# Gate and up of three feed-forwards as seven block products, token-major, in a two-layer hybrid decoder trunk

## The chip, the cores and the metric

One core of a Trainium2 chip runs the whole program as one launch. The metric is the device time of one execution in microseconds (us); the comparisons use medians of runs. The engines are TensorE (PE, matmuls; PEld is its weight load), VectorE (DVE), ScalarE (ACT), GpSimd (POOL) and SyncE (SP), which here only issues DMAs. Each works through its own queue in order and waits for the others by semaphores.

## The reference

Two layers over 512 tokens of width 1024, all in float32. The change concerns `swiglu_ffn`, which runs twice per layer:

```python
for l in range(DEPTH):                                   # DEPTH = 2
    h = rmsnorm(x, ffn1_norm[l])
    x = x + 0.5 * swiglu_ffn(h, ffn1_w_gate[l], ffn1_w_up[l], ffn1_w_down[l])
    h = rmsnorm(x, mix_norm[l])                          # S5 scan, pooling, convolution
    ...
    x = x + y @ w_out[l]
    h = rmsnorm(x, xattn_norm[l])
    x = x + cross_attention(h, rmsnorm(mem, mem_norm[l]), ...)
    h = rmsnorm(x, ffn2_norm[l])
    x = x + 0.5 * swiglu_ffn(h, ffn2_w_gate[l], ffn2_w_up[l], ffn2_w_down[l])
return rmsnorm(x, final_norm)

def swiglu_ffn(h, w_gate, w_up, w_down):                 # 1024 -> 2816 -> 1024
    return (jax.nn.silu(h @ w_gate) * (h @ w_up)) @ w_down
```

## The kernel before

Every float32 product is made of three matmuls on rounded parts (`mm3`, L249 to L252): high x high, high x low and low x high. The high part of a tile is a copy on ACT, the low part a subtraction on DVE. `wload` (L237) does that for weights: a DMA on SP's queue into `raw` (three buffers), a copy to `wh` (L241) and a subtraction to `wl` (L243) on DVE, or on POOL where `eng` says so.

`Norm` (L165) makes the input of each stage. `half` (L183) is called when half a token tile of x is final: a square with a sum on ACT, the mean on DVE (L190), the power -1/2 on POOL (L191, one column), then `emit` (L195): the gain product on DVE (L197), four 128x128 transposes on PE (L200) into a bank of the pool `ax` (two banks), and the high and low parts (L201 on ACT, L202 on DVE). `prep` loads the gain. The result is x transposed: 128 rows of the width by 512 tokens, eight of them.

`ffn` (L320) goes over the 22 column tiles of 128 of the inner width. `gate_up` (L326) keeps a 128x128 block of weights still and moves 512 tokens: 8 blocks of the width x 3 passes for the gate (`pgffn`) and the same for up (`puffn`). The first tile does it by halves of the tokens (`proj_halves`, 256 columns), so that it can begin when two token tiles are normed. Sigmoid, two multiplications (L336 to L338) and a split (L257, L259) give h, with the inner width on the partitions, as `down` (L341) needs it: in three passes of 6 tiles, token tiles of h stay still and 512 columns of the down weights move (`pdffn`), and the sum is added to x on DVE (L317). The last 4 tiles go in `finish` (L353, `plffn`), token tile by token tile, so that the next norm starts on tile 0 while PE is on tile 1.

The stages run in the order ffn1, mix, att, ffn2 for each layer. The S5 matrices of a layer are built in the background of its own ffn1 (`s5_build`, L377), for the most part on POOL, into twelve tiles of the pool C, which the mixer reads. PSUM has 8 banks: 5 in the pool `mm`, 2 in `ax`, 1 named `cacc`. Order within each engine's queue is set when the program is built: a planner takes the instructions that its own model of time holds ready, those that come earlier in the program first, and gives them buffers from the pools.

Of the kernel before, what the change touches and what calls it, by code (L numbers as in the profile page):

```python
# [9 lines left out]
F32 = mybir.dt.float32  # L10
# [7 lines left out]
P = 128  # L18
# [26 lines left out]
def trunk_kernel(ctx: ExitStack, tc: tile.TileContext, io, out, phases=None):  # L45
# [119 lines left out]
    class Norm:  # L165
# [17 lines left out]
        def half(self, t, h):  # L183
            if h == 0:
                self.ss[t] = small(f"ss_{self.name}{t}", (P, 4))
            ss = self.ss[t]
            sq = bt(f"sq_{self.name}{t}{h}")
            A.activation(out=sq, in_=xt[t][:, dsl(h)], func=AF.Square, scale=D ** -0.5, accum_out=ss[:, h:h + 1])
            if h == 1:
                V.tensor_scalar(out=ss[:, 2:3], in0=ss[:, 0:1], scalar1=ss[:, 1:2], scalar2=EPS, op0=ADD, op1=ADD)  # L190
                G.tensor_tensor(out=ss[:, 3:4], in0=ss[:, 2:3], in1=nhalf[:, 0:1], op=ALU.pow)  # L191
                for i in range(2):
                    self.emit(t, i, ss[:, 3:4])

        def emit(self, t, h, r):  # L195
            xn = bt(f"xn_{self.name}{t}{h}")
            V.scalar_tensor_tensor(out=xn, in0=xt[t][:, dsl(h)], scalar=r, in1=self.gb[h], op0=MUL, op1=MUL)  # L197
            ps = ax(f"xp_{self.name}{t}{h}", (P, NK // 2, P))
            for k in range(NK // 2):
                T.transpose(ps[:, k, :], xn[:, k * P:(k + 1) * P], ident)  # L200
            A.activation(out=self.hl[0][h][:, :, tsl(t)], in_=ps, func=AF.Copy)  # L201
            V.tensor_tensor(out=self.hl[1][h][:, :, tsl(t)], in0=ps, in1=self.hl[0][h][:, :, tsl(t)].bitcast(F32), op=SUB)  # L202

# [116 lines left out]
    def ffn(which, l, norm, nxt, bg):  # L320
# [40 lines left out]
        for p, (f0, n) in enumerate(zip(starts, sizes)):  # L361
            for i in range(n):
# [5 lines left out]
                next(bg, None)  # L368
# [4 lines left out]


    s5m = {}

    def s5_build(l):  # L377
# [93 lines left out]
        G.tensor_tensor(out=bbh, in0=bh, in1=zrb, op=MUL)  # L471
        G.tensor_tensor(out=tmp, in0=btl, in1=zib, op=MUL)
        G.tensor_tensor(out=bbh, in0=bbh, in1=tmp, op=ADD)
        G.tensor_tensor(out=bbt, in0=btl, in1=zrb, op=MUL)
        G.tensor_tensor(out=tmp, in0=bh, in1=zib, op=MUL)
        G.tensor_tensor(out=bbt, in0=bbt, in1=tmp, op=SUB)
# [22 lines left out]
        vsb = st(f"vsb{l}", (P, NG, GK))  # L499
        for f in range(NS):  # L500
            minT = ct_(f"minT{l}_{f}", (P, GF, P))
            vps = ax(f"vps{l}_{f}", (P, GF, GK))
            for hf in range(2):
# [11 lines left out]
                G.tensor_tensor(out=gt, in0=bc_m(bbh), in1=bc_p(pg, 0), op=MUL)  # L515
                G.tensor_tensor(out=t_, in0=bc_m(bbt), in1=bc_p(pg, 1), op=MUL)
                G.tensor_tensor(out=gt, in0=gt, in1=t_, op=ADD)
# [5 lines left out]
                A.activation(out=minT[:, hf * 4:hf * 4 + 4, :], in_=tps, func=AF.Copy)  # L523
# [3 lines left out]
            mout = ct_(f"mout{l}_{f}", (P, GF, CH, GK))  # L527
            for hf in range(2):
                g0 = f * GF + hf * 4
                mo = mout[:, hf * 4:hf * 4 + 4, :, :]  # L530
                t_ = st(f"mtt{l}_{f}{hf}", shp)
                G.tensor_tensor(out=mo, in0=bc_m(chat), in1=bc_p(pm, 0), op=MUL)
                G.tensor_tensor(out=t_, in0=bc_m(ctil), in1=bc_p(pm, 1), op=MUL)
                G.tensor_tensor(out=mo, in0=mo, in1=t_, op=ADD)
            yield
            toep = ct_(f"toep{l}_{f}", (P, GF, CH, GK))
            for hf in range(2):
                ti = st(f"toepi{l}_{f}{hf}", (P, 4, GF, GK))
                G.memset(ti, 0.0)
# [3 lines left out]
                A.activation(out=toep[:, :, hf * 4:hf * 4 + 4, :].rearrange("q g i k -> q i g k"), in_=ti, func=AF.Copy)  # L543

            tab = ct_(f"tab{l}_{f}", (P, 2, GF, NC))
            c_, s_ = tab[:, 0, :, :], tab[:, 1, :, :]
            G.memset(tab[:, 0, :, 0:1], 1.0)
            G.memset(tab[:, 1, :, 0:1], 0.0)
            ta = st(f"ta{l}_{f}", (P, 2, GF, NC // 2))
            for q in range(6):  # L550
# [16 lines left out]

    def mixer(l, norm, nxt):
# [19 lines left out]
        mats, rho = s5m.pop(l)  # L588
# [413 lines left out]
    for i, (kind, l) in enumerate(phases):  # L1002
        nxt = norm_for(i + 1)
        if kind == "ffn1":
            def bg():
                if l == 0:
                    yield from prepare()
                yield from s5_build(l)
            ffn("ffn1", l, cur, nxt, bg())
# [4 lines left out]
        else:  # L1014
            ffn("ffn2", l, cur, nxt, iter(()))
# [22 lines left out]
```

## Time and profile before

| | |
|---|---|
| median of 3 runs | 2153.11 us (2147.66 to 2153.69) |
| profiled execution | 2154.13 us, span of its instructions 2152.3 us |
| busy: PE, DVE, ACT, POOL | 2103.0, 1154.4, 724.4, 426.3 us |
| mean granted TensorE clock | 0.989 of full speed |
| instructions: PE, DVE, ACT, POOL | 10132, 1743, 1105, 496 |
| DMA | 217.22 MB, mean 101 GB/s |

Times in the rows count from the span's first instruction. The four feed-forwards lie at about 17 to 398, 725 to 1089, 1089 to 1460 and 1785 to 2147 us. Matmuls overlap each other, so that the distance of their starts, not the duration of one, is what PE needs.

### The profile page before, as it was taken

How to read it: one execution, taken by the hardware profiler on the slowest of the kernel's cores; microseconds unless marked ns; L12 is line 12 of the kernel's file. 1: busy time of each engine (PE TensorE's matmuls, PEld its weight loads, DVE VectorE, ACT ScalarE, POOL GpSimd, SP SyncE). 2: the span in 40 equal slices, each digit the busy share in tenths (PEclk: the TensorE clock that was granted, in tenths of full speed). 3: DMA queues.
4: the chain of work that ended last, by engine and by line, in shares of the span. 5: the costliest groups of instructions: out<-in, count | busy, mean ns of one | idle time of the engine just before them, and what ended most of it. 6: DMA issues, size and time to landing. Idle time of an engine off the chain costs nothing.

```text
span 2152.3 us, 25954 instructions
## 1 busy us (share of the span) xinstructions
PE 2103.0 (98%) x10132; PEld 1765.3 (82%) x10132; DVE 1154.4 (54%) x1743; ACT 724.4 (34%) x1105; POOL 426.3 (20%) x496
## 2 busy tenths in 40 slices
PE   7999999999999999999999999999999999999998
PEld 6888888888787888888888888888877878888887
DVE  5654444599654543344475444446996445433443
ACT  4523233434343322222343232234344423222222
POOL 0217412566100000000023571014550000000000
PEclk9999999999999999999999999999999999999999
DMA  5433334244322233333413323342433213233341
GB/s 161 115 111 94 88 104 145 77 119 131 105 88 79 59 98 98 98 98 108 128 46 112 103 94 100 102 127 87 124 121 111 78 60 97 93 96 97 98 124 62
DMA packets 313521, 217.22 MB, mean 101 GB/s; under 512 B 31566, under 2 KB 275000, under 8 KB 313400
## 3 DMA queue, kind: packets, MB, share of 16 engines
q1 hardware_dynamic: 312736, 214.51, 33.1%
q8 instruction: 79, 1.29, 0.2%
q10 hardware_dynamic: 664, 1.07, 0.1%
q14 instruction: 42, 0.34, 0.1%
HBM read 207.48 MB, written 6.29 MB: 99 GB/s over the span
## 4 chain that ended last, share of the span: by engine, by line
PE 89%; DVE 6%; ACT 1%; DMA 1%; issue 1%; POOL 0%; SPq 0%; DVEq 0%; POOLq 0%; ACTq 0%
PE pgffn L250 7%; PE pgffn L251 7%; PE pgffn L252 7%; PE puffn L252 7%; PE puffn L250 7%; PE puffn L251 7%; PE pdffn L250 6%; PE pdffn L252 6%; PE pdffn L251 6%; DVE cacc L737 1%; PE qps L251 1%; PE qps L252 1%; PE qps L250 1%; PE pwo L250 1%; PE pwo L251 1%; PE pwo L252 1%
## 5 line engine op out<-in xcount | busy, mean ns | idle before, releaser
L250 PE MATMUL pgffn<-xh_ffn,wh_gffn 128*128 128x512 f32 (+1 forms) x720 | 277.1, 385 | 0.6 <-ACT xh_ffn L201 0.5
L251 PE MATMUL pgffn<-xl_ffn,wh_gffn 128*128 128x512 f32 (+1 forms) x720 | 276.5, 384 | 0.0
L250 PE MATMUL puffn<-xh_ffn,wh_uffn 128*128 128x512 f32 (+1 forms) x720 | 275.5, 383 | 0.0
L251 PE MATMUL puffn<-xl_ffn,wh_uffn 128*128 128x512 f32 (+1 forms) x720 | 275.5, 383 | 0.0
L252 PE MATMUL puffn<-xh_ffn,wl_uffn 128*128 128x512 f32 (+1 forms) x720 | 275.4, 382 | 0.0
L252 PE MATMUL pgffn<-xh_ffn,wl_gffn 128*128 128x512 f32 (+1 forms) x720 | 275.3, 382 | 0.0
L243 DVE TENSOR_TENSOR wl_uffn<-wr_uffn,wh_uffn 128x1024 fp32r<-128x1024 f32 x87 | 107.5, 1236 | 261.2 <-ACT wh_uffn L241 261.2
L251 PE MATMUL pdffn<-wl_dffn,h_ffffn 128*128 128x512 f32 x576 | 224.2, 389 | 0.0
L252 PE MATMUL pdffn<-wh_dffn,l_ffffn 128*128 128x512 f32 x576 | 224.2, 389 | 0.0
L250 PE MATMUL pdffn<-wh_dffn,h_ffffn 128*128 128x512 f32 x576 | 223.7, 389 | 0.5 <-DVE sffn L337 0.5
L241 ACT ACTIVATE wh_uffn<-wr_uffn 128x1024 fp32r<-128x1024 f32 x87 | 92.1, 1059 | 262.7 <-issue 163.5
L241 ACT ACTIVATE wh_gffn<-wr_gffn 128x1024 fp32r<-128x1024 f32 x87 | 92.0, 1058 | 252.0 <-issue 133.9
L338 DVE TENSOR_TENSOR sffn<-puffn,sffn 128x512 f32<-128x512 f32 x88 | 60.8, 691 | 208.6 <-PE puffn L252 208.3
L243 DVE TENSOR_TENSOR wl_dffn<-wr_dffn,wh_dffn 128x1024 fp32r<-128x1024 f32 x72 | 101.3, 1408 | 115.1 <-ACT wh_dffn L241 115.1
L241 ACT ACTIVATE wh_dffn<-wr_dffn 128x1024 fp32r<-128x1024 f32 x72 | 76.3, 1060 | 253.0 <-issue 164.7
L250 PEld LDWEIGHTS pgffn<-xh_ffn,wh_gffn 128*128 128x128 f32 x720 | 135.3, 188 | 27.2 <-ACT xh_ffn L201 1.5
L251 PEld LDWEIGHTS puffn<-xl_ffn,wh_uffn 128*128 128x128 f32 x720 | 135.4, 188 | 26.4
L251 PEld LDWEIGHTS pgffn<-xl_ffn,wh_gffn 128*128 128x128 f32 x720 | 135.4, 188 | 26.3 <-DVE xl_ffn L202 0.6
L252 PEld LDWEIGHTS pgffn<-xh_ffn,wl_gffn 128*128 128x128 f32 x720 | 135.4, 188 | 26.4 <-DVE wl_gffn L243 0.2
L250 PEld LDWEIGHTS puffn<-xh_ffn,wh_uffn 128*128 128x128 f32 x720 | 135.4, 188 | 26.3
L252 PEld LDWEIGHTS puffn<-xh_ffn,wl_uffn 128*128 128x128 f32 x720 | 135.4, 188 | 26.1
L243 DVE TENSOR_TENSOR wl_gffn<-wr_gffn,wh_gffn 128x1024 fp32r<-128x1024 f32 x87 | 115.6, 1329 | 49.8 <-ACT wh_gffn L241 49.6
(440 smaller groups left out, 4186.4 us busy)
## 6 DMA issues: line engine op xcount, KB each, us to landing
wr_gffn<-in_ffn_w_gate_dram SPq DMA_DIRECT2D x87, 512.0 KB
wr_uffn<-in_ffn_w_up_dram SPq DMA_DIRECT2D x87, 512.0 KB
wr_dffn<-in_ffn_w_down_dram SPq DMA_DIRECT2D x72, 512.0 KB
wr_lastffn<-in_ffn_w_down_dram SPq DMA_DIRECT2D x16, 512.0 KB
wr_k<-in_xattn_wk_dram SPq DMA_DIRECT2D x16, 512.0 KB
wr_v<-in_xattn_wv_dram SPq DMA_DIRECT2D x16, 512.0 KB
wr_q<-in_xattn_wq_dram SPq DMA_DIRECT2D x16, 512.0 KB
wr_xo<-in_xattn_wo_dram SPq DMA_DIRECT2D x16, 512.0 KB
```

The lines of the kernel that those rows point to most:

```text
L241: A.activation(out=h, in_=raw, func=AF.Copy)
L243: (eng or V).tensor_tensor(out=lo, in0=raw, in1=h.bitcast(F32), op=SUB)
L250: T.matmul(ps, lhsT=wh, rhs=ah, start=first, stop=False, skip_group_check=skip)
L251: T.matmul(ps, lhsT=wh, rhs=al, start=False, stop=False, skip_group_check=skip)
L252: T.matmul(ps, lhsT=wl, rhs=ah, start=False, stop=last, skip_group_check=skip)
L338: V.tensor_tensor(out=s, in0=ps[1], in1=s, op=MUL)
L737: V.scalar_tensor_tensor(out=acc[:, d:], in0=h[:, 0:S - d], scalar=cw[:, TAPS - 1 - d:TAPS - d], in1=acc[:, d:], op0=MUL, op1=ADD)
```

## The change

The second, third and fourth feed-forward use `ffn7` in place of `ffn`; the first stays. There, [gate, up] is one product of two-by-two blocks: x is cut into token halves and width halves, the weights into width halves and gate / up. Seven products of blocks (numbered 1, 2, 5, 6, 3, 7, 4 in their order) with sums of blocks before and after take the place of eight. `PairNorm` makes the seven left factors: the gain product as before, differences and sums of token tiles t and t + 2 on DVE (`combine`), then four transposes and a split for each of seven factors and two token tiles (`give`). A unit is four column tiles of 128 (the last unit has two). Its gate and up weights come in four quarters of 128 x 4 x 512, each with two DMAs of 512 KB. Sums of quarters are made on DVE, in the first unit on POOL, there behind the last `pow` of the norm for all but the first sum (`mix1`, `mix2`, `mix3`). A product holds 128 tokens of x still and moves 512 weight columns, 24 matmuls for two token tiles in two banks: x and y in `mm`, z in `ax`. Results are copied out on ACT (`keep`) or added on DVE (`join`). After products 3 and 7 + 4 the gate of one token half follows, with tokens on the partitions; `turn` transposes this h on PE through the one bank `cacc`, four transposes for each token tile and unit. Down runs unit by unit, in two steps (columns 0 to 511 and 512 to 1023) that stand ahead of the last product of the next unit; the last unit's part goes token tile by token tile at the end. Weights of a step are split two steps ahead.

Both layers' S5 matrices are built in the first feed-forward: layer 0 as before on POOL into C, layer 1 on DVE into smaller tiles that go to memory. The second mixer loads them back, which leaves C free for weights and factors in between. The core of the diff:

```diff
+    class PairNorm(Norm):
...
+        def take(self):
+            for kh, z in ((0, 0), (1, 0), (0, 1), (1, 1)):
+                self.raw[kh, z] = quarter(self.w[z], kh, z, 0, 4 * P, f"first_{self.name}")
...
+            for i, z in ((1, "h"), (2, "l"), (5, "h"), (6, "l")):
+                t2 = xgp.tile([P, 2, HK, HS], F32R, tag=f"x{z}", name=f"xc_{self.name}{i}")
+                self.xg[i] = (t2[:, 0], t2[:, 1])
+            for i in (3, 7, 4):
+                self.xg[i] = tuple(ct_(f"xc{z}_{self.name}{i}", (P, HK, HS), F32R) for z in "hl")
...
+        def emit(self, t, h, r):
+            xn = self.xn[t, h] = (bt if h else vc)(f"xn_{self.name}{t}{h}")
+            V.scalar_tensor_tensor(out=xn, in0=xt[t][:, dsl(h)], scalar=r, in1=self.gb[h], op0=MUL, op1=MUL)
+            if t < 2:
+                self.give(t, h + 1, xn)
+            elif h == 1:
+                s1 = self.xn[t, 2] = (vc if t == 2 else bt)(f"xs_{self.name}{t}")
+                V.tensor_tensor(out=s1, in0=xn, in1=self.xn[t, 0], op=SUB)
+                self.marks = self.give(t - 2, 5, s1)
+
+        def combine(self, i):
+            for tp in range(2):
+                a11, a12, a21, a22, s1 = (self.xn[z] for z in ((tp, 0), (tp, 1), (tp + 2, 0), (tp + 2, 1), (tp + 2, 2)))
+                if i == 6:
+                    V.tensor_tensor(out=a21, in0=a11, in1=a21, op=SUB)
+                    V.scalar_tensor_tensor(out=a11, in0=s1, scalar=-1.0, in1=a11, op0=MUL, op1=SUB)
+                elif i == 3:
+                    V.scalar_tensor_tensor(out=a12, in0=a12, scalar=-1.0, in1=a11, op0=MUL, op1=SUB)
+                self.give(tp, i, {6: a11, 3: a12, 7: a21, 4: a22}[i])
+
+        def give(self, tp, i, src):
+            ps = ax(f"xp_{self.name}{tp}{i}", (P, HK, P))
+            for k in range(HK):
+                T.transpose(ps[:, k, :], src[:, k * P:(k + 1) * P], ident)
+            h, lo = (z[:, :, tsl(tp)] for z in self.xg[i])
+            return [A.activation(out=h, in_=ps, func=AF.Copy).ins,
+                    V.tensor_tensor(out=lo, in0=ps, in1=h.bitcast(F32), op=SUB).ins]
...
+    def ffn7(which, l, norm, nxt):
+
+
+        wg, wu, wd = (io[f"{which}_w_{n}"][l] for n in ("gate", "up", "down"))
+        units = [(f, min(4, NF - f)) for f in range(0, NF, 4)]
...
+                self.eng = V if u else G
...
+            def mix1(self):
+                a, b = self.raw[0, 0], self.raw[0, 1]
+                t1 = self.raw["t1"] = [vt(f"wt_{self.nm}{k}", (P, self.W)) for k in range(HK)]
+                for k in range(HK):
+                    self.eng.tensor_tensor(out=t1[k], in0=a[k // 2][:, k % 2, :], in1=b[k // 2][:, k % 2, :], op=ADD)
+
+            def sum_(self, to, other):
+                for a, b in zip(self.raw[to], self.raw[other]):
+                    self.eng.tensor_tensor(out=a, in0=b, in1=a, op=ADD)
+
+            def mix2(self):
+                self.sum_((0, 1), (1, 1))
+                self.sum_((0, 0), (0, 1))
+
+            def mix3(self):
+                self.sum_((1, 0), (0, 0))
+
+            def product(self, c, i, first, last, src, post):
+                ps = self.ps
+
+                def run(w):
+                    if first:
+                        ps[c] = [(ax if c == "z" else mm)(f"p{c}{self.nm}{t}", (P, self.W)) for t in range(2)]
+                    h, lo = norm.xg[i]
+                    for k in range(HK):
+                        for t in range(2):
+                            mm3(ps[c][t], h[:, k, tsl(t)], lo[:, k, tsl(t)], w[k][0], w[k][1], first and k == 0,
+                                k == HK - 1, True)
+                    for t in range(2):
+                        post(t)
+                steps.append((run, lambda: split2(self.raw[src], f"{self.nm}p{i}")))
...
+            def gate(self, t, half, g, nu):
+                sg = bt(f"sg{self.nm}{half}{t}", (P, self.W))
+                A.activation(out=sg, in_=g, func=AF.Sigmoid)
+                V.tensor_tensor(out=sg, in0=g, in1=sg, op=MUL)
+                V.scalar_tensor_tensor(out=nu, in0=sg, scalar=-1.0, in1=nu, op0=MUL, op1=MUL)
+                later.append(lambda: self.turn(2 * half + t, nu))
+
+            def turn(self, t, src):
+                pt = cx(f"ht{self.nm}{t}", (P, self.nf, P))
+                for i in range(self.nf):
+                    T.transpose(pt[:, i, :], src[:, i * P:(i + 1) * P], ident)
+                if self.nf <= 2:
+                    hl = bt(f"hhl{self.nm}{t}", (P, 2, self.nf, P), F32R)
+                    h, lo = hl[:, 0], hl[:, 1]
+                else:
+                    h, lo = (bt(f"h{z}{self.nm}{t}", (P, self.nf, P), F32R) for z in "hl")
+                A.activation(out=h, in_=pt, func=AF.Copy)
+                V.tensor_tensor(out=lo, in0=pt, in1=h.bitcast(F32), op=SUB)
+                self.ht[t] = (h, lo)
...
+                def run(w):
+                    for t in range(NT):
+                        ps = mm(f"pd{name}{t}")
+                        hh, hl = self.ht[t]
+                        for i in range(self.nf):
+                            mm3(ps, hh[:, i, :], hl[:, i, :], w[i][0], w[i][1], i == 0, i == self.nf - 1)
+                        add_x(t, dh, ps, 0.5)
+
...
+            un.product("x", 1, True, False, (0, 0), un.keep("x", "u1"))
+            un.product("y", 2, True, True, (1, 0), un.join("y", "u1"))
+            un.product("z", 5, True, False, "t1", un.keep("z", "u5"))
+            un.product("x", 6, False, False, (0, 0), un.keep("x", "u2"))
+            un.product("z", 3, False, True, (1, 1),
+                       un.join("z", "u2", lambda t, un=un: un.gate(t, 0, un.e["u1", t], un.e["u2", t])))
+            un.product("x", 7, False, False, (0, 1), un.join("x", "u5"))
...
+            if u == 0:
+                for j, i in enumerate((6, 3, 7, 4)):
+                    when(j + 1, lambda i=i: norm.combine(i))
+            lead = 2 if u == 0 else 0
+            when(-lead, un.mix1)
+            if u == 0:
+                def behind(f):
+                    with tc.issue_after(norm.pow):
+                        f()
+                when(1 - lead, lambda: behind(us[0].mix2))
+                when(2 - lead, lambda: behind(us[0].mix3))
+            else:
+                when(1, un.mix2)
+                when(2, un.mix3)
+            final = u + 1 == len(us)
+            if u > 0:
+                us[u - 1].down(0)
+                if not final:
+                    us[u - 1].down(1)
+            if not final:
+                nu_ = us[u + 1]
...
+            un.product("x", 4, False, True, (1, 0),
+                       lambda t, un=un: un.gate(t, 1, un.ps["x"][t], un.e["u5", t]))
+            if final and u > 0:
+                us[u - 1].down(1)
...
+            if 0 <= i + 2 < n:
+                with ExitStack() as es:
+                    if 2 <= i + 2 < 7:
+                        for z in norm.marks:
+                            es.enter_context(tc.issue_after(z))
+                    w[i + 2] = steps[i + 2][1]()
+            if i < 0:
+                continue
+            now, later[:] = later[:], []
+            steps[i][0](w.pop(i))
+            for f in now:
+                f()
+        nxt.prep()
+        for f in later:
+            f()
+        un = us[-1]
...
+    def s5_build(l, kept):
+        E = G if kept else V
...
+        def put(i, sl, t):
+            if not kept:
+                nc.sync.dma_start(out=sl(spill[f][i]), in_=t)
...
-        mats, rho = s5m.pop(l)
+        mats, rho, spill = s5m.pop(l)
+        if spill is not None:
+            mats = [[ct_(f"sl{l}_{f}{i}", shape) for i, shape in enumerate(MATS)] for f in range(NS)]
+            for f in range(NS):
+                for i in range(len(MATS)):
+                    nc.sync.dma_start(out=mats[f][i], in_=spill[f][i])
...
+    def seven(i):
+        return i > 0 and phases[i][0] in ("ffn1", "ffn2")
...
-                if l == 0:
+                if i == 0:
                     yield from prepare()
-                yield from s5_build(l)
-            ffn("ffn1", l, cur, nxt, bg())
+                    for k in range(L):
+                        yield from s5_build(k, k == 0)
+            if seven(i):
+                ffn7(kind, l, cur, nxt)
+            else:
+                ffn(kind, l, cur, nxt, bg())
-            ffn("ffn2", l, cur, nxt, iter(()))
+            ffn7(kind, l, cur, nxt)
```

## Rows read from the trace of the kernel before

**Rows 1.** The page's first part: busy us (share of the span) xinstructions of each engine.

```profile
PE 2103.0 (98%) x10132; PEld 1765.3 (82%) x10132; DVE 1154.4 (54%) x1743; ACT 724.4 (34%) x1105; POOL 426.3 (20%) x496
```

**Rows 2.** Waits of PE: who waited for whom, total us, times, longest.

```profile
PE xp_ffn L200 <- DVE xn_ffn L197: 10.5, 1, 10.5
...
PE xp_ffn L200 <- DVE xl_ffn L202: 4.9, 4, 2.6
```

**Rows 3.** Windows: length, busy us (count) PE, PEld, DVE, ACT, POOL, PEclk, DMA, GB/s.

```profile
724.00:730.00 6.00, 6.00 (x49) 5.80 (x48) 5.88 (x10) 2.95 (x6) 0.54 (x1) 1.00 0.64 182
730.00:736.00 6.00, 5.75 (x46) 5.20 (x45) 2.41 (x4) 1.09 (x2) 0.00 (x0) 1.00 0.29 83
...
850.00:900.00 50.00, 50.00 (x223) 41.40 (x222) 19.92 (x24) 14.06 (x18) 0.00 (x0) 1.00 0.30 95
...
1250.00:1300.00 50.00, 50.00 (x229) 41.53 (x228) 28.38 (x22) 13.48 (x17) 42.43 (x84) 1.00 0.28 87
...
1500.00:1550.00 50.00, 48.60 (x288) 43.10 (x287) 48.22 (x76) 18.10 (x26) 29.51 (x18) 0.96 0.42 119
```

**Rows 4.** Timeline of PE: start, duration; two 512-column matmuls 24 starts apart.

```profile
799.99 0.39 PE L252 MATMUL puffn<-xh_ffn,wl_uffn 128*128 128x512 f32 x1
...
805.43 0.39 PE L252 MATMUL pdffn<-wh_dffn,l_ffffn 128*128 128x512 f32 x1
```

**Rows 5.** Timeline of PE: two 256-column matmuls 8 starts apart.

```profile
1094.04 0.29 PE L250 MATMUL pgffn<-xh_ffn,wh_gffn 128*128 128x256 f32 x1
...
1095.00 0.28 PE L252 MATMUL pgffn<-xh_ffn,wl_gffn 128*128 128x256 f32 x1
```

**Rows 6.** Timeline of PE: eight transposes between two matmuls (second one left out).

```profile
711.64 0.39 PE L251 MATMUL pwo<-wl_xo,h_o 128*128 128x512 f32 x1
711.87 1.03 PE L200 MATMUL xp_ffn<-ident,xn_ffn 128*128 128x128 f32 x8
...
712.98 0.40 PE L250 MATMUL pwo<-wh_xo,h_o 128*128 128x512 f32 x1
```

**Rows 7.** Groups of PE by form: count, busy us, mean ns, idle before.

```profile
L250 PE MATMUL pgffn<-xh_ffn,wh_gffn 128*128 128x512 f32 x672 | 263.3, 392 | 0.0
...
L251 PE MATMUL pdffn<-wl_dffn,h_ffffn 128*128 128x512 f32 x576 | 224.2, 389 | 0.0
```

**Rows 8.** Timeline of PE at the boundary from attention to the second feed-forward.

```profile
724.99 0.28 PE L250 MATMUL pgffn<-xh_ffn,wh_gffn 128*128 128x256 f32 x1
...
731.60 1.04 PE L200 MATMUL xp_ffn<-ident,xn_ffn 128*128 128x128 f32 x8
732.88 0.38 PE L250 MATMUL pgffn<-xh_ffn,wh_gffn 128*128 128x256 f32 x1 [0.25 <-ACT xh_ffn L201]
```

**Rows 9.** Timeline of DVE and ACT near 1061 to 1097, queues of back-to-back operations.

```profile
1061.09 1.23 DVE L243 TENSOR_TENSOR wl_uffn<-wr_uffn,wh_uffn 128x1024 fp32r<-128x1024 f32 x1 [3.61 <-ACT wh_uffn L241]
1062.23 0.68 DVE L337 TENSOR_TENSOR sffn<-pgffn,sffn 128x512 f32<-128x512 f32 x1
...
1082.33 0.69 DVE L202 TENSOR_TENSOR xl_ffn<-xp_ffn,xh_ffn 128x512 fp32r<-128x512 f32 x1 [0.99 <-ACT xh_ffn L201]
...
1083.53 0.68 DVE L202 TENSOR_TENSOR xl_ffn<-xp_ffn,xh_ffn 128x512 fp32r<-128x512 f32 x1
...
1085.40 1.42 DVE L197 SCALAR_TENSOR_TENSOR xn_ffn<-x,ss_ffn,gb_ffn 128x512 f32<-128x512 f32 x2 [0.71 <-POOL ss_ffn L191]
...
1097.51 0.60 ACT L201 ACTIVATE xh_ffn<-xp_ffn 128x512 fp32r<-128x512 f32 x1 [0.56 <-PE xp_ffn L200]
```

**Rows 10.** DVE and POOL side by side: two timeline rows, two groups (mean ns).

```profile
1263.02 2.36 DVE L243 TENSOR_TENSOR wl_dffn<-wr_dffn,wh_dffn 128x1024 fp32r<-128x1024 f32 x1 [0.24 <-ACT wh_dffn L241]
...
1263.02 1.28 POOL L517 TENSOR_TENSOR gt<-gt,gtt 128x512 f32<-128x512 f32 x1
...
L338 DVE TENSOR_TENSOR sffn<-puffn,sffn 128x512 f32<-128x512 f32 x3 | 2.1, 692 | 7.3 <-PE puffn L252 7.3
...
L243 POOL TENSOR_TENSOR wl_v<-wr_v,wh_v 128x1024 fp32r<-128x1024 f32 x22 | 54.0, 2464 | 31.4 <-ACT wh_v L241 24.7 <-PE kps L252 6.1 <-DMA sys<-sdy 0.5
```

More of the change, by code (lines that the diff above doesn't have):

```diff
@@ L190, in half @@
                 V.tensor_scalar(out=ss[:, 2:3], in0=ss[:, 0:1], scalar1=ss[:, 1:2], scalar2=EPS, op0=ADD, op1=ADD)
[L191 removed]
+                self.pow = G.tensor_tensor(out=ss[:, 3:4], in0=ss[:, 2:3], in1=nhalf[:, 0:1], op=ALU.pow).ins
                 for i in range(2):
@@ L367, in ffn @@
                     kept.append(keep_rows(wd, fl + i, f"last{which}{l}_{i}", st if i < 3 else vc))
-                next(bg, None)
+                for _ in range(2):
+                    next(bg, None)
         for _ in bg:
@@ L375, in trunk_kernel, with quarter @@
+    def quarter(w, kh, z, c0, W, name):
+        got = []
+        for s in range(2):
+            r = (wp.tile([P, 2, W], F32, tag="raw", name=f"wr_{name}{kh}{z}{s}") if (kh, z) == (1, 1) else
+                 ct_(f"wr_{name}{kh}{z}{s}", (P, 2, W)))
+            r0 = (kh * HK + 2 * s) * P
+            nc.sync.dma_start(out=r, in_=w[r0:r0 + 2 * P, c0:c0 + W].rearrange("(k p) c -> p k c", p=P))
+            got.append(r)
+        return got
     s5m = {}
-    def s5_build(l):
+    MATS = ((P, GF, P), (P, GF, CH, GK), (P, GF, CH, GK), (P, 2, GF, NC))
@@ L499, in s5_build, with whole, half @@
         vsb = st(f"vsb{l}", (P, NG, GK))
+        def whole(name, shape):
+            return ct_(f"{name}{l}_{f}", shape) if kept else None
+        def half(tile_, sl, name, shape):
+            return sl(tile_) if kept else st(f"{name}{l}_{f}", shape)
+        def put(i, sl, t):
+            if not kept:
+                nc.sync.dma_start(out=sl(spill[f][i]), in_=t)
+        spill = None if kept else [[drp.tile(list(shape), F32, tag=f"m{f}{i}", bufs=1, name=f"sm{l}_{f}{i}")
+                                    for i, shape in enumerate(MATS)] for f in range(NS)]
         for f in range(NS):
-            minT = ct_(f"minT{l}_{f}", (P, GF, P))
+            minT = whole("minT", MATS[0])
             vps = ax(f"vps{l}_{f}", (P, GF, GK))
@@ L522, in s5_build @@
                     T.matmul(vps[:, hf * 4 + g, :], lhsT=gg, rhs=chat[:, g0 + g, :], start=True, stop=True)
-                A.activation(out=minT[:, hf * 4:hf * 4 + 4, :], in_=tps, func=AF.Copy)
+                hsl = slice(hf * 4, hf * 4 + 4)
+                mh = half(minT, lambda z: z[:, hsl, :], f"minT{hf}", (P, 4, P))
+                A.activation(out=mh, in_=tps, func=AF.Copy)
+                put(0, lambda z: z[:, hsl, :], mh)
                 yield
@@ L542, in s5_build @@
                     nc.sync.dma_start(out=ti[0:rows, i, :, :], in_=vsb[P - rows:P, gsl, :])
[L543 to L548, printed above, removed]
+                th = half(toep, lambda z: z[:, :, hsl, :], f"toep{hf}", (P, GF, 4, GK))
+                A.activation(out=th.rearrange("q g i k -> q i g k"), in_=ti, func=AF.Copy)
+                put(2, lambda z: z[:, :, hsl, :], th)
+            tab = whole("tab", MATS[3])
+            c_, s_ = (half(tab, lambda z: z[:, i, :, :], f"tab{i}", (P, GF, NC)) for i in range(2))
+            E.memset(c_[:, :, 0:1], 1.0)
+            E.memset(s_[:, :, 0:1], 0.0)
             ta = st(f"ta{l}_{f}", (P, 2, GF, NC // 2))
@@ L987, in norm_for @@
         kind, l = phases[i]
+        if seven(i):
+            return PairNorm(f"{kind}{l}", io[gains[kind]][l], *(io[f"{kind}_w_{z}"][l] for z in ("gate", "up")))
         return Norm(f"{kind}{l}", io[gains[kind]][l])
+    def seven(i):
+        return i > 0 and phases[i][0] in ("ffn1", "ffn2")
     cur = norm_for(0)
```

156 lines of the change are left out of this document (131 added, 25 removed).

## The prediction

> **What bounds the kernel now.** I read four views, from coarse to fine. The page's first part says who is busy: PE 98% of the span, VectorE (DVE) 54%, ScalarE (ACT) 34%, GpSimd (POOL) 20% [rows 1]. A busy PE need not be a full one, so the next view is what PE waited for: the longest sum is 10.5 us at the start of the program, and of the feed-forwards only 4.9 us of norm transposes at their four starts stand high [rows 2]. The windows then show the stages apart: in the middle of a feed-forward PE is busy 50.00 of 50 us at a granted clock of 1.00, with DVE at 19.92; in the mixer DVE is at 48.22 and PE loses 1.4 us at 0.96 [rows 3]. Last, the timeline gives the pace at which matmuls start, which is what a pipelined engine costs: 24 matmuls of 512 columns in 805.43 - 799.99 = 5.44 us, 0.2267 us each [rows 4]; 8 of 256 columns in 0.96 us, 0.120 us each [rows 5]. The 0.39 us of a single one overlaps its neighbours and isn't used. So a feed-forward ends when PE has issued its columns, and DVE and ACT are hidden. By these prices one feed-forward, with 1536 full and 96 half matmuls and 32 transposes (priced below), is 348.2 + 11.5 + 3.6 = 363.3 us of PE.
>
> **The matmuls.** Before, gate and up take 22 column tiles x 2 x 8 x 3 = 1056 matmuls per feed-forward; tile 0 runs them as halves, so it is 1008 full and 96 half ones (672 full ones for each line of gate over four feed-forwards, 168 in each [rows 7]): 228.5 + 11.5 = 240.0 us. After, a unit of four column tiles has 7 products x 4 k x 2 token tiles x 3 passes = 168 matmuls; 22 tiles are five units of 512 columns and one of 256: 840 x 0.2267 + 168 x 0.120 = 190.4 + 20.2 = 210.6 us. Gain 29.4 us. That stationary and moving operand change places costs nothing: down already moves weights, at the same 0.389 us each [rows 7]. Down keeps its 528 matmuls.
>
> **The transposes.** Eight of 128x128 stand between two full matmuls: 712.98 - 711.64 - 2 x 0.2267 = 0.887 us, 0.111 us each [rows 6]. The norm goes from 32 to 7 x 2 x 4 = 56, and h adds 22 x 4 = 88, so 112 more: 12.4 us on PE, where nothing hides them. Net 17.0 us per feed-forward, 51.0 us for three. The profiled execution took 2154.1 us, of which 2152.3 is the span, so PE alone would give 2103.1. What follows is how much of this is given back, because DVE has to stay ahead.
>
> **DVE in a usual unit.** Prices by start-to-start: a 1024-column subtraction 1.14 us, a 512-column one 0.60, a gain product 0.71 [rows 9]. A product's weights are one 1024 and two 512 pieces: 2.34, seven times 16.4. Weight sums 4 x 0.60 + 6 x 1.14 = 9.2. Six joins 3.6, gates 8 x 0.60 = 4.8, the low part of h 2.4. Two down steps 2 x 2.34 + 8 x 0.60 = 9.5. Sum 45.9 us beside PE's 168 x 0.2267 + 96 x 0.2267 + 16 x 0.111 = 61.6: 75%, where it was 40% [rows 3]. In order: from the start of product 1 to product 7, PE needs 5 x 5.44 = 27.2 us, and DVE has to finish some 27 of work by then with two products already split; the two down steps (21.8 us of PE, 9.5 of DVE) let it recover. I take 2.5 us per feed-forward for all units after the first, with ends 0 and 10 (each of the 22 new h transposes waits for bank cacc, 0.45 us of a 0.69 us DVE op each).
>
> **DVE in the first unit.** Here the norm stands in front. In the present boundary the first matmul of the feed-forward starts at 724.99, and the last transposes only at 731.60, hidden because the first tokens' matmuls fill the time; PE then waits 0.25 us [rows 8]. After, products 1 and 2 (10.9 us) need only tokens 0 to 255 and cover this. DVE, from 724 on: norm rest 8.3 (5.88 + 2.41 [rows 3]), differences and sums of the pairs 5.4 with eight low parts 4.8 less two that go 1.2, splits of products 5, 6, 3, 7, 4 11.8, joins 3.6, gate and turn 3.8, the next unit's two splits 4.7: 41.2 us, and PE's 7 x 5.44 + 32 x 0.111 = 41.6. There is no slack left. The weight sums of this unit are on POOL, and six of 1024 columns stand behind the last norm's pow: 6 x 2.46 = 14.8 us [rows 10], just in time for product 6 at 16.4 us. A DVE subtraction that started with a POOL op at 1263.02 took 2.36 us where 1.23 is usual [rows 9, 10]. About nine such DVE ops fall into POOL's 14.8 us; at 1.1 us each that is 10 us, of which I take half, as many start in a gap: **5 us** per feed-forward, ends 0 and 15. Product 7's transposes need an ax bank that product 5 and 3 hold; they come 0.69 + 0.44 + 0.60 + 0.69 = 2.4 us after product 3, inside these ends.
>
> The Trainium skill, "SBUF — State Buffer", section "SBUF: two separate sides", says that DVE with two SBUF inputs and POOL share a port pair as an exclusive lock, the loser being blocked for the whole instruction. The 2.36 us agrees with it. By that rule POOL's whole 14.8 us would be lost to DVE, which is the second rival.
>
> **The ends of the feed-forwards.** The last pass over down has 48 matmuls in place of 96: 10.9 us of PE and 1.8 of transposes beside DVE's 4 tiles x (2 x 0.60 + 0.21 + 1.42 + 2 x 0.60) = 16.1. Towards another feed-forward products 1 and 2 cover it; towards the mixer only 48 halves, 5.8 us, do; the final norm loses about 1. I take 3 us for all, ends 0 and 8. **The S5 matrices.** Both layers are now built in the first feed-forward, the second on DVE. POOL spent 42.43 of 50 us on one layer in its fullest window [rows 3]; in all it is 426.3 us busy in the program [rows 1], of which I put 100 on one layer, as an estimate, and half of that on DVE, whose 512 columns take 0.60 where POOL's 1.28 [rows 9, 10]. That is 50 us more in a stage with DVE about half idle: 3 us, ends 0 and 10. PE's part only moves. The 12 matrices (512 KB each) go to memory and back through SP's queue, ahead of the mixer's weights; 6.3 MB at 182 GB/s [rows 3] is 35 us each way, hidden by the last unit and by the 50 us to the scan; without cover it is the fourth rival. The 4 MB of first weights that a boundary now loads are 23 us at that rate, beside the last part of attention or the last unit.
>
> **Sum.** 3 x 5 + 3 x 2.5 + 3 + 3 = 28.5 given back: 2103.1 + 28.5 = 2131.6 by the profiled execution, which is 1.0 above the median of the runs: **2131 us**.
>
> **Rivals.** (1) The cover holds everywhere: the first unit's 41.2 fits because the planner puts next-unit matmuls into the gaps; give-back 0 to 7 us, 2105. For it: DVE was never late in a feed-forward. Against: 41.2 of 41.6. (2) The port decides, and it ends on the slower side: in the first unit DVE stands still for all of POOL's 14.8 us, so 3 x 15 + 13.5 = 58.5 are given back: 2161. It is slower from 57.5 us given back on, faster below 44.5. For it: the 2.36 us; against: DVE ops that read PSUM keep 0.69 beside a busy POOL [rows 10]. (3) PE, which waits for weights alone today, now waits 4 times a unit for the h bank (ACT 0.60 + DVE 0.69 [rows 9], more behind a full DVE queue): 2 us for each of 11 pairs, 22 per feed-forward in place of 2.5, 2131 + 58 = 2189, down to 2170. Against: the transposes stand a product behind their source. (4) The S5 build or the reload costs: 20 us in the first feed-forward or at the second mixer, 2150.
>
> **Numbers.** Forecast 0.51 (2110 to 2146), cover 0.12, port 0.18, h bank 0.09, S5 0.10. A measurement here can tell about 0.3% from no change, 6.5 us: faster is below 2146.7, slower above 2159.6. Faster 0.51 + 0.12 + 0.03 of S5 + 0.02 of port = 0.68; same 0.05 + 0.06 = 0.11; slower 0.10 of port, 0.09, 0.02 = 0.21. Range 2104 to 2172.
>
> **What would show it.** Product groups of 24 matmuls 5.44 us long; 256-column ones at 0.120; feed-forwards of 340 to 355 us in place of some 363; PE's waits listed under the low parts of weights and of x in the first unit; DVE near 75%. It is wrong if 512-column matmuls start further apart than 0.23 us, if the usual units lose more than 3 us each, or if the mixer of layer 1 starts late on a load.

## The result

| | before | after |
|---|---|---|
| median | 2150.7 us | 2169.2 us |
| ratio to before, 95% interval | | 1.0084 [1.0061, 1.0108] |
| profiled execution's span | 2152.3 us | 2168.9 us |
| mean granted TensorE clock | 0.989 | 0.978 |

The changed kernel is 0.8% slower; 2131 us was forecast, and faster. The page of the changed kernel, its first part (busy us, share of the span, instructions):

```profile
PE 2074.1 (96%) x10180; PEld 1737.9 (80%) x10180; DVE 1574.8 (73%) x2562; ACT 916.0 (42%) x1528; POOL 387.5 (18%) x361
```

Against [rows 1] PE is 29 us less busy, where 51 us were forecast, and it stands idle for 95 us of the span in place of 49. The busy time at full clock shows most of the saving: the second feed-forward before, and in the experiment with memsets below, which has the changed kernel's matmuls (columns as in [rows 3]):

```profile
724.76:1088.74 363.98, 363.73 (x1665) 303.29 (x1664) 156.31 (x190) 104.07 (x141) 2.16 (x4) 1.00 0.34 102
```

```profile
737.41:1089.98 352.57, 348.61 (x1665) 290.91 (x1664) 272.22 (x399) 165.22 (x275) 17.98 (x19) 1.00 0.32 100
```

PE is 15 us less busy there, of 17 forecast. The waits of PE in the changed kernel (total us, times, longest), to be held against [rows 2]:

```profile
PE xp_ffn L249 <- DVE xc_ffn L252: 22.7, 4, 8.9
...
PE xp_ffn L249 <- DVE xs_ffn L233: 4.8, 3, 1.9
```

L249 to L252 are `give`: the transposes of the factors and their split. Both waits are new, and both stand in the first units. The windows there (columns as in [rows 3]), from the second feed-forward's start at 737, and at the end one of its middle:

```profile
737.00:752.00 15.00, 12.61 (x61) 10.07 (x59) 14.49 (x12) 3.22 (x7) 11.09 (x5) 1.00 0.00 0
752.00:762.00 10.00, 1.54 (x5) 1.03 (x5) 9.93 (x9) 3.12 (x6) 5.99 (x3) 0.52 0.00 1
762.00:767.00 5.00, 4.47 (x15) 3.32 (x16) 5.00 (x9) 3.25 (x8) 0.00 (x0) 0.60 0.00 0
767.00:792.00 25.00, 24.17 (x118) 19.37 (x117) 18.54 (x27) 17.35 (x28) 0.00 (x0) 1.00 0.51 169
850.00:900.00 50.00, 50.00 (x228) 41.35 (x227) 39.12 (x55) 25.07 (x37) 0.00 (x0) 1.00 0.40 127
```

From 752 to 762 PE works 1.54 us, DVE is busy nearly all the time, POOL up to 758, and the granted clock reads 0.52 and then 0.60: PE goes on at half clock for a while. In the middle of the feed-forward PE is busy 50.00 of 50 us and DVE 39.12: there the change does what was forecast. What DVE and POOL do at that place, from the timeline (start, duration):

```profile
741.81 5.67 DVE L228 SCALAR_TENSOR_TENSOR xn_ffn<-x,ss_ffn,gb_ffn 128x512 f32<-128x512 f32 x2 [0.44 <-POOL ss_ffn L191]
747.41 0.68 DVE L252 TENSOR_TENSOR xc_ffn<-xp_ffn,xc_ffn 128x512 fp32r<-128x512 f32 x1
748.01 2.26 DVE L233 TENSOR_TENSOR xs_ffn<-xn_ffn,xn_ffn 128x512 f32<-128x512 f32 x1
750.30 2.73 DVE L240 TENSOR_TENSOR xn_ffn<-xn_ffn,xn_ffn 128x512 f32<-128x512 f32 x1
753.06 2.73 DVE L241 SCALAR_TENSOR_TENSOR xn_ffn<-xs_ffn,xn_ffn 128x512 f32<-128x512 f32 x1
755.82 2.71 DVE L243 SCALAR_TENSOR_TENSOR xn_ffn<-xn_ffn,xn_ffn 128x512 f32<-128x512 f32 x1
...
741.75 16.24 POOL L476 TENSOR_TENSOR wr_first_ffn<-wr_first_ffn,wr_first_ffn 128x1024 f32<-128x1024 f32 x6
```

This is the reading that decides the case. POOL's six sums take 16.24 us, 2.71 each. In nearly the same time DVE gets through six operations with two inputs from SBUF, 2.26 to 2.83 us each (the first two together 5.67), where the same forms take 0.68 to 0.71 elsewhere ([rows 9], and below). The one that reads PSUM (L252) takes its usual 0.68. The two engines take turns. The shut-out operations are the last of the norm (`emit`, L228, L233) and the sums of `combine` (L240 to L243), on which the factors of products 5, 6 and 3 hang.

By stages, from the first and last matmuls of each in the timelines (each from the end of the stage before; the first from 17 us on):

| us | before | after |
|---|---|---|
| first feed-forward | 381.0 | 399.6 |
| first mixer, attention | 200.6, 126.2 | 195.3, 124.9 |
| second feed-forward | 363.9 | 363.5 |
| third, to the mixer's first matmul | 373.3 | 371.0 |
| second mixer, attention | 196.0, 124.9 | 199.9, 124.8 |
| fourth | 362.2 | 363.1 |
| after the last matmul | 7.2 | 9.8 |

The three changed feed-forwards should have come to some 346 us each; each gives back all of its 17 us; the third also holds the 4.3 us before the mixer's first matmul. The first is 18.6 us longer, of which 9.4 is PE's work of the second S5 build that moved there (373.3 - 363.9 before).

### The profile page after: what moved, and what is told of

Read it like the earlier page. It is cut to its first block, busy times and chain, and to the rows that moved or that the text cites. A ratio compares the mean times of both kernels' runs of the same rounds, so it can differ in the third digit from the quotient of the medians.

```text
span 2168.9 us, 27451 instructions
## 1 busy us (share of the span) xinstructions
PE 2074.1 (96%) x10180; PEld 1737.9 (80%) x10180; DVE 1574.8 (73%) x2562; ACT 916.0 (42%) x1528; POOL 387.5 (18%) x361
## 3 DMA queue, kind: packets, MB, share of 16 engines
q10 hardware_dynamic: 664, 1.07, 0.1%
## 4 chain that ended last, share of the span: by engine, by line
PE 79%; DVE 14%; ACT 2%; DMA 2%; issue 2%; SPq 0%; POOL 0%; DVEq 0%; POOLq 0%; ACTq 0%
PE pxffn L301 5%; PE pxffn L302 5%; PE pxffn L300 5%; PE pddffn L301 5%; PE pddffn L302 5%; PE pddffn L300 5%; DVE cacc L1052 3%; PE pzffn L300 3%; PE pzffn L301 3%; PE pzffn L302 3%; PE pgffn L301 2%; PE pgffn L300 2%; PE pgffn L302 2%; PE puffn L302 2%; PE puffn L300 2%
## 5 line engine op out<-in xcount | busy, mean ns | idle before, releaser
L301 PE MATMUL pddffn<-wl_dffn,hhffn 128*128 128x512 f32 x480 | 188.9, 394 | 0.0
L302 PE MATMUL pddffn<-wh_dffn,hlffn 128*128 128x512 f32 x480 | 188.2, 392 | 0.0
L300 PE MATMUL pddffn<-wh_dffn,hhffn 128*128 128x512 f32 x480 | 185.8, 391 | 0.0
L1052 DVE SCALAR_TENSOR_TENSOR cacc<-ch,convw,cacc 128x510 f32<-128x510 f32 (+28 forms) x174 | 127.9, 735 | 5.7 <-ACT cacc L1050 2.0
L367 DVE SCALAR_TENSOR_TENSOR x<-pddffn,x 128x512 f32<-128x512 f32 x120 | 82.5, 687 | 66.6 <-PE pddffn L302 66.6
L301 PEld LDWEIGHTS pddffn<-wl_dffn,hhffn 128*128 128x128 f32 x480 | 90.2, 188 | 18.3
L302 PEld LDWEIGHTS pddffn<-wh_dffn,hlffn 128*128 128x128 f32 x480 | 90.2, 188 | 17.9
L300 PEld LDWEIGHTS pddffn<-wh_dffn,hhffn 128*128 128x128 f32 x480 | 89.8, 188 | 18.4
L476 DVE TENSOR_TENSOR wr_ffn<-wr_ffn,wr_ffn 128x1024 f32<-128x1024 f32 (+1 forms) x90 | 98.5, 1112 | 0.1
L300 PE MATMUL pdffn<-wh_dffn,h_ffffn 128*128 128x512 f32 x144 | 57.0, 396 | 1.5 <-DVE sffn L387 1.5
```

Source lines behind the costliest of these rows:

```text
L300: T.matmul(ps, lhsT=wh, rhs=ah, start=first, stop=False, skip_group_check=skip)
L301: T.matmul(ps, lhsT=wh, rhs=al, start=False, stop=False, skip_group_check=skip)
L302: T.matmul(ps, lhsT=wl, rhs=ah, start=False, stop=last, skip_group_check=skip)
L367: V.scalar_tensor_tensor(out=x_, in0=ps, scalar=scale, in1=x_, op0=MUL, op1=ADD)
L476: self.eng.tensor_tensor(out=a, in0=b, in1=a, op=ADD)
L1052: V.scalar_tensor_tensor(out=acc[:, d:], in0=h[:, 0:S - d], scalar=cw[:, TAPS - 1 - d:TAPS - d], in1=acc[:, d:], op0=MUL, op1=ADD)
```

## The experiments

Two theories stood at the start. **Port:** POOL's additions shut DVE out, and this makes the loss at the first units and part of that in the first feed-forward. **Load or chain:** the first unit has as much DVE work as PE work, and the chain from norm to factors is too long, whatever POOL does. All kernels are the changed kernel with one edit, unless said otherwise; ratios are to the kernel before.

**The six sums on DVE.**

```diff
-                    self.eng.tensor_tensor(out=a, in0=b, in1=a, op=ADD)
+                    V.tensor_tensor(out=a, in0=b, in1=a, op=ADD)
...
-                when(1 - lead, lambda: behind(us[0].mix2))
-                when(2 - lead, lambda: behind(us[0].mix3))
+                when(1 - lead, us[0].mix2)
+                when(2 - lead, us[0].mix3)
```

> In the first unit of the three changed feed-forwards the six 1024-column sums of weight quarters are made on DVE in place of POOL (the first four sums stay on POOL); nothing else is changed. Port theory (a POOL addition shuts DVE's operations with two SBUF inputs out for its whole length): these DVE operations take 0.6 to 0.7 us again where the changed kernel shows 2.7, DVE has 6.8 us more to do in each first unit, PE's longest wait there falls from 8.9 us to under 4, and the time to some 2142 us, below the kernel before. Load theory (the first unit simply has more DVE work than PE work): another 6.8 us of it make it worse, 2170 to 2190 us.

Measured 2141.3 us, ratio 0.9954 [0.9939, 0.9969]. More work on DVE, and 28 us less time: with it the change is a gain. The edit does two things: it gives the sums to the other engine, and it drops the order that kept them behind the norm's last power. Dropping the order alone is worth 19 us ("The sums wherever the planner puts them"), so these 28 us are not the engine's alone; the memset experiment separates the two. The same DVE operations in its timeline:

```profile
741.31 1.41 DVE L228 SCALAR_TENSOR_TENSOR xn_ffn<-x,ss_ffn,gb_ffn 128x512 f32<-128x512 f32 x2 [0.45 <-POOL ss_ffn L191]
742.64 0.68 DVE L243 SCALAR_TENSOR_TENSOR xn_ffn<-xn_ffn,xn_ffn 128x512 f32<-128x512 f32 x1
743.24 0.68 DVE L233 TENSOR_TENSOR xs_ffn<-xn_ffn,xn_ffn 128x512 f32<-128x512 f32 x1
743.96 0.69 DVE L240 TENSOR_TENSOR xn_ffn<-xn_ffn,xn_ffn 128x512 f32<-128x512 f32 x1
```

PE's wait for the factors fell from 22.7 us to 3.9 in total:

```profile
PE xp_ffn L249 <- DVE xc_ffn L252: 3.9, 3, 1.4
```

**The six sums left out.** The edit removes the two calls.

```diff
-                when(1 - lead, lambda: behind(us[0].mix2))
-                when(2 - lead, lambda: behind(us[0].mix3))
+                pass
```

> The six 1024-column sums of weight quarters in the first unit of the three changed feed-forwards are left out, so products 6, 7 and 4 of that unit use unsummed weights; all else is as in the changed kernel. Port theory: without POOL beside it DVE keeps up, the loss of about 17 us at each first unit shrinks to 2 to 5 us, 2125 to 2135 us. Load or chain theory (DVE's own 41 us in that unit, or the chain from transposes over copies to low parts): neither changes, PE still waits about 9 us, 2160 to 2170 us.

Measured 2135.8 us, 0.9926 [0.9911, 0.9941], just above what the port theory gave. The second feed-forward takes 351.9 us here and the fourth 352.6, 5.6 and 6.3 more than PE's own 346.3. So the load and the chain cost about 6 us per feed-forward; the other 11 of the 17 ((2169.2 - 2135.8) / 3) go with POOL's sums. On DVE, without the order, the sums cost 2 ((2141.3 - 2135.8) / 3). The windows of the same stretch:

```profile
738.00:753.00 15.00, 13.23 (x66) 10.70 (x64) 12.83 (x21) 5.12 (x10) 0.87 (x1) 1.00 0.00 1
753.00:763.00 10.00, 9.19 (x42) 7.19 (x43) 9.27 (x14) 7.67 (x14) 0.00 (x0) 1.00 0.18 54
```

PE works 9.19 of the 10 us in which it had 1.54, and the clock stays at 1.00: the half clock followed the stall and is not there without it.

**POOL busy, but not reading.** Zeros written twice in place of each sum.

```diff
-                    self.eng.tensor_tensor(out=a, in0=b, in1=a, op=ADD)
+                    if self.eng is V:
+                        V.tensor_tensor(out=a, in0=b, in1=a, op=ADD)
+                        continue
+                    for _ in range(2):
+                        G.memset(a, 0.0)
```

> In place of each of the six POOL sums of the first units (two inputs from SBUF) POOL writes zeros into the same tile, twice, so that it is busy for about as long at the same places and in the same order of dependences; the sums are left out, and products 6, 7 and 4 of the first unit use zeros. If DVE is held off by POOL's reads, its operations there take 0.6 to 0.7 us and the time is that of the kernel without the sums, 2136 us. If any work of POOL on SBUF does it, or the order in which the planner puts them, PE's wait of 8.9 us stays, 2160 us or more.

Measured 2132.7 us, 0.9914 [0.9897, 0.9930]. Its timeline at the same place, DVE and POOL:

```profile
742.44 1.42 DVE L228 SCALAR_TENSOR_TENSOR xn_ffn<-x,ss_ffn,gb_ffn 128x512 f32<-128x512 f32 x2 [0.44 <-POOL ss_ffn L191]
...
744.51 0.68 DVE L233 TENSOR_TENSOR xs_ffn<-xn_ffn,xn_ffn 128x512 f32<-128x512 f32 x1
745.22 0.69 DVE L240 TENSOR_TENSOR xn_ffn<-xn_ffn,xn_ffn 128x512 f32<-128x512 f32 x1
...
742.36 10.81 POOL L480 MEMSET wr_first_ffn<- 128x1024 f32 x12
```

POOL is busy for 10.81 us from the same point on, the order behind the norm's last power is kept, and DVE does not notice. So the loss is due neither to POOL's being busy nor to that order by itself. Nor is it the length of an instruction alone: a memset takes 0.90 us (10.81 / 12), and the sums of the next experiment, 1.07 us each (25.59 / 24), do stretch DVE. The Trainium skill, "SBUF — State Buffer", section "SBUF: two separate sides", says just this: the shared ports are a lock for the whole instruction, and a DVE operation with two SBUF inputs contends only with a POOL operation that reads SBUF. The rows agree on each point.

**Finer pieces on POOL.** 24 sums of 256 columns in place of six of 1024.

```diff
-                    self.eng.tensor_tensor(out=a, in0=b, in1=a, op=ADD)
+                    if self.eng is V:
+                        V.tensor_tensor(out=a, in0=b, in1=a, op=ADD)
+                        continue
+                    for k in range(2):
+                        for c in range(0, self.W, 256):
+                            G.tensor_tensor(out=a[:, k, c:c + 256], in0=b[:, k, c:c + 256], in1=a[:, k, c:c + 256],
+                                            op=ADD)
```

> The same POOL sums in the first unit, cut from six of 1024 columns into twenty-four of 256. Port theory: a DVE operation then waits at most some 0.6 us in place of 2.1, so DVE operations of 2.7 us fall to about 1.3; POOL's sums are spread over a longer stretch, about 25 us in place of 16; the time lies between, 2145 to 2160 us. Load theory: no change, 2165 to 2172 us.

Measured 2146.4 us, 0.9965 [0.9950, 0.9980], with single times from 2137 to 2147. The loss is mostly gone although POOL does the same sums in the same order. The profiled run is the fastest of them (2137.2 us):

```profile
738.45 2.36 DVE L228 SCALAR_TENSOR_TENSOR xn_ffn<-x,ss_ffn,gb_ffn 128x512 f32<-128x512 f32 x2 [0.44 <-POOL ss_ffn L191]
...
742.05 1.11 DVE L240 TENSOR_TENSOR xn_ffn<-xn_ffn,xn_ffn 128x512 f32<-128x512 f32 x1
...
738.39 25.59 POOL L481 TENSOR_TENSOR wr_first_ffn<-wr_first_ffn,wr_first_ffn 128x256 f32<-128x256 f32 x24
```

A DVE operation takes 1.11 to 1.18 us beside these pieces, in place of some 2.7: what it pays grows with the length of one POOL instruction. The last sum ends later than in the changed kernel (25.59 us after the first began, in place of 16.24), and the time is still 23 us less, so it is not late sums that made the loss. Why the single times spread stays open. A new wait, for the first weights, may be the price of the later sums:

```profile
PE pxffn L300 <- ACT wh_ffn_0p L441: 8.0, 2, 4.0
```

**Two of the six sums on DVE.**

```diff
+            def mix3v(self):
+                for a, b in zip(self.raw[1, 0], self.raw[0, 0]):
+                    V.tensor_tensor(out=a, in0=b, in1=a, op=ADD)
...
-                when(2 - lead, lambda: behind(us[0].mix3))
+                when(2 - lead, us[0].mix3v)
```

> Of the six POOL sums of the first units the last two (those for product 4) are made on DVE, four stay on POOL. If the cost goes with the time that POOL reads while DVE is needed, two thirds of the loss of 28 us stay or somewhat more, as the first four come when DVE is needed most: 2155 to 2165 us. If one POOL sum behind the norm were enough to upset the order, 2169 us.

Measured 2161.0 us, 1.0041 [1.0026, 1.0056]: 20 of the 28 us stay with four sums of six, and two thirds of PE's wait for the factors (22.7 us before the edit):

```profile
PE xp_ffn L249 <- DVE xc_ffn L252: 15.4, 5, 6.0
```

The cost goes with the number of sums that stay behind the norm on POOL.

**The sums wherever the planner puts them.**

```diff
-                when(1 - lead, lambda: behind(us[0].mix2))
-                when(2 - lead, lambda: behind(us[0].mix3))
+                when(1 - lead, us[0].mix2)
+                when(2 - lead, us[0].mix3)
```

> The changed kernel with its POOL sums of the first units, but without the order that puts them behind the norm's last power; the planner may start them as soon as their data are there. Port theory: what of them runs while PE still has the stage before costs little, the rest as much as now; a power may wait some 2 us behind a sum: 2150 to 2168 us. If the place of the sums were what makes the loss and not POOL's port, moving them would either cure it (2136) or change nothing.

Measured 2150.4 us, 0.9994 [0.9984, 1.0004]: no better than the kernel before, but 19 us better than the changed kernel with all sums still on POOL. So the place of the sums counts too. By stages the third feed-forward falls to 358.7 us and the fourth to 355.8, while the second stays at 362.8. The second has two losses left: its last two sums still stand beside gain products (2.89 and 2.28 us, from 738 on), and all six sums of the third feed-forward now run in the second's last unit, where they stretch subtractions of weights:

```profile
PE pddffn L300 <- DVE x L367: 4.7, 1, 4.7
...
1073.53 5.51 POOL L476 TENSOR_TENSOR wr_first_ffn<-wr_first_ffn,wr_first_ffn 128x1024 f32<-128x1024 f32 x2 [3.03 <-DVE wl_ffn_0p L443]
...
1073.91 2.88 DVE L452 TENSOR_TENSOR wl_ffn_0p<-wr_first_ffn,wh_ffn_0p 128x512 fp32r<-128x512 f32 x1
1076.71 2.88 DVE L608 TENSOR_TENSOR wl_lastffn<-wr_lastffn,wh_lastffn 128x512 fp32r<-128x512 f32 x1
...
1083.99 0.68 DVE L367 SCALAR_TENSOR_TENSOR x<-pddffn,x 128x512 f32<-128x512 f32 x1
```

PE waits 4.7 us there for the addition at 1083.99, which stands behind the stretched operations in DVE's queue. The turn-taking is the same; what it costs depends on what PE needs from DVE at that time.

**Both S5 builds on DVE.**

```diff
-        E = G if kept else V
+        E = V
```

> Both layers' S5 matrices are built on DVE in the first feed-forward (in the changed kernel layer 0 is on POOL, layer 1 on DVE). The first feed-forward of the changed kernel takes 18.6 us longer than before, about 9 of them PE work that moved there. Port theory: without POOL beside it the other 9 shrink by about 5 although DVE gets some 50 us more work, 2162 to 2166 us. Load theory: DVE becomes late more often there, 2172 to 2185 us.

Measured 2158.5 us, 1.0036 [1.0022, 1.0050], 10.7 us less than the changed kernel, and less than either theory gave. A stretch of the first feed-forward in the changed kernel, with DVE's subtractions of gate weights in it, then the same of this one:

```profile
100.00:150.00 50.00, 46.79 (x210) 38.67 (x211) 33.51 (x68) 13.79 (x22) 42.22 (x64) 0.93 0.31 92
...
L293 DVE TENSOR_TENSOR wl_gffn<-wr_gffn,wh_gffn 128x1024 fp32r<-128x1024 f32 x2 | 5.6, 2778 | 5.2 <-ACT wh_gffn L291 5.2
```

```profile
100.00:150.00 50.00, 50.00 (x242) 41.59 (x241) 42.17 (x127) 14.49 (x23) 0.00 (x0) 1.00 0.34 101
...
L293 DVE TENSOR_TENSOR wl_gffn<-wr_gffn,wh_gffn 128x1024 fp32r<-128x1024 f32 x2 | 2.4, 1223 | 1.1 <-ACT wh_gffn L291 1.1
```

With POOL busy for 42.22 of 50 us a subtraction of gate weights took 2.78 us on the mean, and PE lost 3.2 us and clock; with all of it on DVE, DVE is busier (42.17 against 33.51), its subtractions take 1.22, and PE loses nothing. The stage falls from 399.6 to 389.8 us, which is before's 381.0 and the 9.4 that moved. That the port does it is read from these rows: no run here keeps POOL busy in this stage without reading. Nor is a busy POOL enough: before, it was busy for 42.43 of 50 us beside a DVE at 28.38, and PE lost nothing [rows 3].

**Both edits together.** The diffs of the first experiment and of the one just above.

> The six sums of the first units on DVE and both layers' S5 matrices built on DVE, everything else as in the changed kernel. If the two losses are both the port's and stand in different stages, they add: 2169 - 28 - 11 = 2130 us, and the ratio to the kernel before is 0.990 to 0.992. If they share a cause that one edit already removes, 2140 us.

Measured 2130.2 us, 0.9905 [0.9888, 0.9921]. The two losses add.

**POOL out of it altogether.** In addition:

```diff
-                self.eng = V if u else G
+                self.eng = V
```

> As the version with the six sums and both S5 builds on DVE, and the first four sums of the first units (512 columns each, made before the norm ends) on DVE too, so that POOL does nothing but the norms' powers in these stages. Port theory: those four lie where PE still has the end of the stage before, so DVE has room either way and the time is the same within 4 us, 2127 to 2135 us.

Measured 2130.3 us, 0.9894 [0.9876, 0.9913]. The four early sums don't matter. This and the version above are the best of the case, 1% below the kernel before.

**Two feed-forwards in place of three, the S5 builds where they were.** With the six sums on DVE; the third feed-forward is the old one, and the background build goes on at its old pace of one step per column tile.

```diff
-                for _ in range(2):
-                    next(bg, None)
+                next(bg, None)
...
-        return i > 0 and phases[i][0] in ("ffn1", "ffn2")
+        return phases[i][0] == "ffn2"
...
-                if i == 0:
+                if l == 0:
                     yield from prepare()
-                    for k in range(L):
-                        yield from s5_build(k, k == 0)
+                yield from s5_build(l, True)
```

> Only the second and fourth feed-forward (both of the kind ffn2) in seven products, with the six sums of the first units on DVE; the third is as in the kernel before, and each layer's S5 matrices are built in their own ffn1 on POOL as before, without the way through memory. By the stages of the version with the sums on DVE a changed ffn2 gains 8.3 and 9.6 us, and nothing is paid in the first feed-forward: 2151 - 18 + 3 for the shorter tail = 2136 us, less than with three changed feed-forwards and POOL in the S5 build (2141). If moving the S5 build cost nothing beyond PE's own work, three are better than two, and this gives 2145 us.

Measured 2140.9 us, 0.9952 [0.9936, 0.9969], the same as with three (2141.3), and between the two forecasts. The changed two take 353.2 and 352.6 us, the first feed-forward 380.3; but the old third one takes 379.5 in place of 373.3. Its waits of PE are 2.9 us there, where the same window before has 0.2:

```profile
PE xp_ffn L200 <- DVE xl_ffn L202: 2.9, 2, 2.0
```

The second feed-forward's last pass over down is shorter now and no longer covers this norm: 32 of its transposes come after that pass, where 16 did before. So with POOL in the S5 build three changed feed-forwards are no better than two: the gain in the third and the cost in the first cancel.

## Why the prediction was wrong

**Right: the prices of PE.** A product in the middle of the second feed-forward, then an h transpose, from the timeline of the changed kernel:

```profile
839.00 0.39 PE L300 MATMUL pxffn<-wh_ffn_1p,xch_ffn 128*128 128x512 f32 x1
...
842.41 0.39 PE L300 MATMUL pddffn<-wh_dffn,hhffn 128*128 128x512 f32 x1
...
843.54 0.39 PE L302 MATMUL pddffn<-wh_dffn,hlffn 128*128 128x512 f32 x1
843.77 0.60 PE L523 MATMUL htffn<-ident,u2ffn 128*128 128x128 f32 x4
...
844.44 0.40 PE L301 MATMUL pddffn<-wl_dffn,hhffn 128*128 128x512 f32 x1
```

15 matmuls in 3.41 us are 0.227 each; four transposes and two matmuls in 0.90 us leave 0.112 for a transpose. The prices that give 17 us per feed-forward hold; as busy time 15 showed above.

**Right, and priced too high: the usual units.** 2.5 us per feed-forward was taken; the whole wait of PE from 800 to 1095 us, in the second feed-forward, is 1.4 us. Rival 3, the one bank for h, did not come: no wait on it stands in the trace.

**Wrong, the step that turned the sign: the first unit.** The prediction had the lock before it in [rows 10], counted nine shut-out operations at 1.1 us, and took half: 5 us. Two things were wrong in it. The wait for one operation grows with the length of POOL's instruction, and POOL's here have 1024 columns: 2.0 us (2.71 - 0.68) for each of six operations, where the row it was priced from stood beside one of 512 (1.28 us) and gave 1.1. And "many start in a gap" was wrong: POOL's sums run back to back, so that there is no gap, and DVE's operations there are the ones that PE waits for. Six times 2.0 is 12, close to the 11 us per feed-forward that go when the sums are left out. PE idles for 12.2 us in the windows from 737 to 792 (55 less 42.8 busy). The other 6 us of the 17 are the load and the chain, for which the first unit had no term of its own: "41.2 in 41.6" was counted as just enough.

Rival 2 (15 us per feed-forward, 0.18) foresaw the sign and nearly the size, as the less likely case; that it came within 2 us is partly luck. It let DVE stand still for all of POOL's 14.8 us and had nothing for the load. In fact DVE got its turns, lost 12 of 16.2 us, and the load added 6.

**Wrong: the S5 build.** 3 us were taken, 9.2 measured (18.6 less 9.4 moved). The price looked at DVE's added work, as if that were the risk; POOL's own build, now dense in the early part of the stage (42.22 of 50 us from 100 to 150), stood beside it, and DVE's operations were stretched. More work on DVE and none on POOL removes the loss.

**Too low: the ends.** 3 us were taken. From the end of the last down matmul of the third feed-forward to the mixer's first are 4.3 us, where before there was no gap, and the tail after the last matmul is 2.6 longer: 7.

The sum, by stages: 54 us given back in the three changed feed-forwards (17.2, 20.4 and 16.8 over 346.3), 9 in the first, 7 at the ends, 3 gained in the mixers and attentions together: 67, less 51 is the 16.6 us between the two spans.

## What to carry to other kernels

Before work goes to POOL to relieve DVE, look at which DVE operations run beside it, and whether the bounding engine waits for them: those with two SBUF inputs paid 2.0 us each beside POOL sums of 1024 columns, so six sums on POOL cost DVE nearly twice what they would have cost on its own queue (12 us against 6 x 1.14 = 6.8). Sums cut into short instructions, or run where PE does not wait for DVE, cost less. A row with a stretched DVE operation is to be scaled with the length of the POOL instruction beside it, not taken over (here 0.4 to 0.5 us beside 256 columns, 1.1 beside 512, 2.0 beside 1024). And a margin of 41.2 in 41.6 us in front of the bounding engine is no cover to take half of a risk from.

## What the hardware showed

The exactness of the turn-taking was not expected: six POOL sums and six DVE operations with two SBUF inputs in some 16.5 us, one for one, while twelve POOL memsets, 10.81 us together, in the same place cost DVE nothing. The clock row was not expected either: in a stretch of 10 us in which PE worked 1.54, the granted clock read 0.52, which is the lower of its two levels (1.2 of 2.4 GHz) nearly throughout, and the 5 us after it 0.60.
